# Second MLP stage in tiles of the first stage's pools, and one written order for its engines

## The chip, the cores and the metric

The kernel runs on one core of a Trainium2 chip. The metric is device time in microseconds, the median of several executions; a profile of one further execution shows where its time goes. Engine names are those of the profile: PE is TensorE (matmuls), PEld its weight loads, DVE is VectorE, ACT is ScalarE, POOL is GpSimd, and SP is SyncE, which issues most transfers.

## The reference

One layer of an encoder with 1024 tokens of width 1024: a normalised input projection, a state-space branch and a neighbourhood attention branch side by side, an output projection with residual, and then the MLP, the only part that the change touches:

```
x = x + jnp.concatenate([y_ssm, y_na.astype(y_ssm.dtype)], axis=-1) @ w_out
h = rmsnorm(x, norm_mlp_w)
return x + jnp.square(jax.nn.relu(h @ w_mlp_in)) @ w_mlp_out     # 1024 -> 4096 -> 1024
```

All of it is float32.

## The kernel before, in words

**Split numbers.** Every matmul operand is split into a high half (ACT copies it to the matmul's rounded type) and a low half (value minus high half, by DVE or POOL; `split_to`, L368 to L370). `chain` (L1218 to L1221) then makes three matmuls of one: high by high, high by low, low by high.

**Seven products.** Both MLP multiplications use a scheme of seven products of half-size blocks instead of eight, in the order `ORD = (1, 2, 6, 5, 7, 3, 4)`. Sums of inputs are made ahead of a product, sums of results behind it. In PSUM, products 1, 6, 7 and 4 add up in the tiles X (`px`), products 2 in Y (`py`), 5 and 3 in a second Y (`pz`).

**First stage** (h @ W1, squared ReLU). Eight blocks `fb` of 512 features (class `Block`). A block loads four weight quarters, and per product: `split` makes the sums of weights (L1583 to L1587) and splits them (ACT high, POOL low); `product` issues 24 matmuls; `sums` copies the PSUM tiles into `cq` (ACT, L1628) or adds them there (DVE, L1633), applies relu and square (ACT, L1638 and L1639, L1630), makes the sums of activations that the second stage needs (DVE, L1646 to L1654) and stores seven forms of the activations to DRAM (`act_dr`; from SP, for the last block from POOL). The transposed input `hc` lives in the pools `hA` and `b0`, the blocks' results in four buffers of `hq`.

**Second stage** (times W2, plus residual). Four parts `fb` of 1024 features. A part loads eight weight quarters into `wraw`, and per product: two loads of activations `ar` from `act_dr`; splits of them into `ahl` (ACT high, DVE low, `a_split`); sums of weights (DVE: L1915 and L1916 for products 6 and 5, L1918 for 7, L1920 for 4); splits of two weights (ACT high, POOL low, L370); 48 matmuls in four groups t of 12; and four adds of a PSUM tile to the accumulators `acc` (DVE, L1945). `acc` is loaded with the residual from `x2_dr`. In the last part finished tiles are stored to the output.

**Pools.** Before, the first stage's pools are closed (`b0s.close()`), and the second stage opens ten pools of its own in their memory. Weight splits go round seven pairs, activation splits round six, activation loads round four tiles.

**Order of work.** The stages before the MLP are emitted by planners that set an order, kept by `in_order` (L1188): each instruction gets a dependency, without a semaphore, on the one emitted before it on the same engine. Blocks 0 to 7 of the first stage and the whole second stage are outside `in_order`: there a scheduler of the language, which works with estimated times, chooses the order of each engine's instructions.

Of the kernel before, what the change touches and what calls it, by code (L numbers as in the profile page):

```python
# [19 lines left out]
P = 128  # L20
T = 1024
D = 1024
# [208 lines left out]
def hymba_block(  # L231
# [136 lines left out]
    def split_to(hl, src, eng):  # L368
        nc.scalar.activation(hl[0], src, AF.Copy)  # L369
        eng.tensor_tensor(hl[1], src, hl[0].bitcast(F32), op=sub)  # L370
# [150 lines left out]
    with ExitStack() as ph:  # L521
# [663 lines left out]
        behind = {}  # L1185

        @contextmanager
        def in_order():  # L1188
            traced = nc.cur_bb.bb.instructions
            mark = traced[-1]  # L1190
            yield
            start = next(i for i in reversed(range(len(traced))) if traced[i] is mark) + 1
            for ins in traced[start:]:
                if ins.engine in behind:
                    tc.add_manual_dep(
                        ins,
                        behind[ins.engine].name,
                        mybir.DependencyInfo(
                            mybir.DependencyClass.NoSync, mybir.DependencyReason.DATA
                        ),  # L1200
                        reason="issue_after",
                    )
                behind[ins.engine] = ins
# [342 lines left out]
    with ExitStack() as ph:  # L1546
# [280 lines left out]
        x2s.close()  # L1827
        arp = arps.enter_context(tc.tile_pool(name="arp", bufs=1, reuse_waits="tile"))
        hq = ph.enter_context(tc.tile_pool(name="hq", bufs=1, reuse_waits="tile"))
        for fb in range(8):  # L1830
            kb = (k0, k1)[fb] if fb < 2 else Block(fb)
            kb.load("12", "21", "22")
            kb.tiles()
            for i in ORD:
                if i not in kb.w:
                    kb.split(i)
                if not (i == 1 and fb < 2 or i == 2 and fb == 0):
                    kb.product(i)
                elif i == 1:
                    kb.to = kb.X  # L1840
                else:
                    kb.to = kb.Y
                kb.sums(i)
    b0s.close()

    with ExitStack() as ph:
        phase["ps"] = ph.enter_context(
            tc.tile_pool(name="ps4", bufs=1, space=PSUM, reuse_waits="tile")
        )
        ra, wa_, rb, x0, wb_, a2, a1, arb = (  # L1850
            ph.enter_context(tc.tile_pool(name=n, bufs=1, side="right", reuse_waits="tile"))
            for n in ("ra", "wa", "rb", "x0", "wb", "a2", "a1", "arb")
        )
        x1, a3 = (
            ph.enter_context(tc.tile_pool(name=n, bufs=1, reuse_waits="tile")) for n in ("x1", "a3")
        )
        acc = [p.tile([P, NT // 2, D], F32, name="acc") for p in (x0, x1)]
        hls[:] = [wa_] * 2 + [wb_] * 2 + [wp] * 3
        raw_a = [arp] * 2 + [ra] * 4
        raw_b = [rb] * 6 + [wp] * 2  # L1860
        raw_x = [arp] * 2 + [arb] * 2
        ahl = [a1] * 2 + [a2] * 2 + [a3] * 2
        for n in ("hl", "raw", "rb", "ar", "ahl"):
            ring[n] = 0

        def raw_of(n):
            if n in ("11", "21"):
                return ring_tile("raw", raw_a, ("wraw",), (F32,))[0]
            return ring_tile("rb", raw_b, ("wraw",), (F32,))[0]

        def a_load(fb, i, u):
            ar = ring_tile("ar", raw_x, ("ar",), (F32,))[0]
            nc.sync.dma_start(
                ar.rearrange("p (a t) -> p a t", a=2), act_dr[fb][i - 1, :, 2 * u : 2 * u + 2, :]
            )
            return ar

        def a_split(ar):
            pool = ahl[ring["ahl"] % 6]
            ring["ahl"] += 1  # L1880
            t = pool.tile([P, 2, 1024], F32R, tag="ahl", name="ahl", bufs=2)
            split_to((t[:, 0], t[:, 1]), ar, nc.vector)
            return t[:, 0], t[:, 1]

        for fb in range(4):
            bq = [{}, {}]
            for n in ("11", "21", "12", "22"):
                for q in bq:
                    q[n] = raw_of(n)
            first = {}  # L1890
            with ExitStack() as order:
                if fb == 1:
                    order.enter_context(tc.issue_after(begun.ins))
                for n in ("11", "21", "12", "22"):
                    for u in range(2):
                        r0 = (2 * fb + u) * 512 + (int(n[0]) - 1) * 256
                        d0 = (int(n[1]) - 1) * 512
                        nc.sync.dma_start(
                            bq[u][n].rearrange("p (a d) -> p a d", a=2),
                            w_mlp_out[0][r0 : r0 + 256, d0 : d0 + 512].rearrange(  # L1900
                                "(a p) d -> p a d", p=P
                            ),
                        )
                    if n in ("11", "21"):
                        i = 1 if n == "11" else 2
                        first[i] = [a_load(fb, i, u) for u in range(2)]
            X = [ps_mm("px2") for _ in range(4)]
            Y = [ps_tp("py2"), ps_tp("py2"), ps_s("py2"), ps_s("py2")]
            for i in ORD:
                wa = []  # L1910
                for u in range(2):
                    q = bq[u]
                    if i == 6:
                        q["t1"], q["t2"] = raw_of("t1"), raw_of("t2")
                        nc.vector.tensor_tensor(q["t1"], q["12"], q["11"], op=sub)  # L1915
                        nc.vector.tensor_tensor(q["t2"], q["22"], q["t1"], op=sub)  # L1916
                    elif i == 7:
                        nc.vector.tensor_tensor(q["12"], q["22"], q["12"], op=sub)  # L1918
                    elif i == 4:
                        nc.vector.tensor_tensor(q["21"], q["21"], q["t2"], op=sub)  # L1920
                    src = q[{1: "11", 2: "21", 3: "22", 4: "21", 5: "t1", 6: "t2", 7: "12"}[i]]
                    ar = first[i][u] if i in first else a_load(fb, i, u)
                    wa.append((a_split(ar), w_split(src, nc.gpsimd)))
                if fb == 0 and i in (1, 6):
                    h = i == 6
                    for t in range(4):
                        begun = nc.sync.dma_start(acc[h][:, t, :], x2_dr[4 * h + t])
                if i == 5:
                    Y = [ps_tp("pz2"), ps_tp("pz2"), ps_s("pz2"), ps_s("pz2")]
                for t in range(4):  # L1930
                    pt = (X if i in (1, 6, 7, 4) else Y)[t]
                    ts = slice(t * P, t * P + P)
                    for u in range(2):
                        (ah, al), (wh, wl) = wa[u]
# [7 lines left out]
                    th, dh = {1: (0, 0), 2: (0, 0), 6: (0, 1), 3: (0, 1), 5: (1, 1), 7: (1, 1), 4: (1, 0)}[i]  # L1942
                    tt = 4 * th + t
                    d = acc[th][:, t, dh * 512 : (dh + 1) * 512]
                    nc.vector.tensor_tensor(d, d, pt, op=add)  # L1945
                    if fb == 3 and i in (2, 7, 3, 4):
                        nc.sync.dma_start(
                            out[0, tt * P : (tt + 1) * P, dh * 512 : (dh + 1) * 512], d
                        )
    arps.close()  # L1950


# [42 lines left out]
```

## Time and profile before

| | |
|---|---|
| time, median of 3 runs | 1585.77 us (1585.5 to 1588.29) |
| profiled execution: its time, its span | 1589.21 us, 1587.4 us |
| mean granted TensorE clock | 0.992 |
| busy: PE, DVE, ACT, POOL | 1548.1, 1013.5, 720.9, 730.3 us |
| HBM read, written | 191.51 MB, 89.18 MB |
| first stage's last block, second stage | from about 1226 us and from 1272.55 us of the span |

The span goes from the first to the last instruction of the profiled execution; its time holds 1.8 us more. A row of a timeline gives start, duration, engine, line, operation, output<-inputs, and in brackets how long the engine was idle before and whose instruction ended that. A row of waits gives the total, the number and the longest.

### The profile page before, as it was taken

The numbers are of one execution on the slowest core, as the hardware profiler recorded it, in microseconds if no ns is written. First come the engines' busy times: TensorE is split into PE (matmuls) and PEld (weight loads), VectorE is DVE, ScalarE is ACT, GpSimd is POOL, SyncE is SP. The second block draws the span as 40 slices with busy tenths as digits, with TensorE's granted clock in tenths as the row PEclk, the third lists the DMA queues.
The fourth block names the chain that finished last, engine by engine and source line by source line (L and its number), as shares of the span: only waits on it lengthen the run. The fifth ranks groups of instructions, "written<-read, shape, count | busy, mean of one in ns | idle before, by whom it ended". The sixth has DMA issues, their size and how long they took to land. (4 is left out here: it accounts for less than half of the span.)

```text
span 1587.4 us, 20805 instructions
## 1 busy us (share of the span) xinstructions
PE 1548.1 (98%) x7462; PEld 1291.3 (81%) x7462; DVE 1013.5 (64%) x1414; ACT 720.9 (45%) x1187; POOL 730.3 (46%) x530
## 2 busy tenths in 40 slices
PE   7999999999999999999999998999999999999999
PEld 5788878888878888788888886888888778888887
DVE  3776444687688854567776475444444579787863
ACT  5444323444345435567686244554454444333330
POOL 2000066774779832233364353444444555555450
PEclk9999999999999999999999999999999989999999
DMA  8212398777777795978792422444443486443332
GB/s 225 54 40 70 89 311 262 231 238 248 230 209 214 225 278 172 257 208 227 193 238 94 159 94 93 174 158 146 151 155 120 159 306 251 159 161 131 107 106 80
DMA packets 184226, 278.73 MB, mean 176 GB/s; under 512 B 14819, under 2 KB 106043, under 8 KB 184123
## 3 DMA queue, kind: packets, MB, share of 16 engines
q1 hardware_dynamic: 133323, 233.88, 48.2%
q10 hardware_dynamic: 49792, 39.85, 7.6%
q0 software_dynamic: 1008, 3.67, 0.6%
q8 instruction: 59, 0.97, 0.3%
q14 instruction: 44, 0.36, 0.1%
HBM read 191.51 MB, written 89.18 MB: 177 GB/s over the span
## 5 line engine op out<-in xcount | busy, mean ns | idle before, releaser
L370 POOL TENSOR_TENSOR wl<-wraw,wh 128x1024 fp32r<-128x1024 f32 x113 | 308.7, 2743 | 305.5 <-ACT wh L369 305.5
L364 PE MATMUL pq<-wh,hTh 128*128 128x512 f32 x512 | 204.9, 400 | 2.3 <-DVE qn L931 1.7
L366 PE MATMUL pq<-wh,hTl 128*128 128x512 f32 x512 | 199.9, 390 | 0.0
L365 PE MATMUL pq<-wl,hTh 128*128 128x512 f32 x512 | 199.7, 390 | 0.1
L369 ACT ACTIVATE wh<-wraw 128x1024 fp32r<-128x1024 f32 x125 | 131.4, 1055 | 143.5 <-PE px L1221 40.1
L1221 PE MATMUL px<-wh,ahl 128*128 128x512 f32 x512 | 163.1, 395 | 4.6 <-ACT ahl L369 3.1
L1221 PE MATMUL px<-h,wh 128*128 128x512 f32 x512 | 160.1, 394 | 2.7 <-DVE cq L1633 2.7
L370 DVE TENSOR_TENSOR ahl<-ar,ahl 128x1024 fp32r<-128x1024 f32 x56 | 117.0, 2094 | 22.4 <-ACT ahl L369 21.5
L369 ACT ACTIVATE ahl<-ar 128x1024 fp32r<-128x1024 f32 x56 | 58.5, 1052 | 160.3 <-PE px L1221 80.6
L1221 PEld LDWEIGHTS px<-wh,ahl 128*128 128x128 f32 x512 | 97.6, 191 | 26.7 <-ACT ahl L369 3.6
L1221 PEld LDWEIGHTS px<-h,wh 128*128 128x128 f32 x512 | 96.6, 190 | 22.9 <-DVE cq L1633 3.1
L364 PEld LDWEIGHTS pq<-wh,hTh 128*128 128x128 f32 x512 | 96.2, 188 | 21.8 <-DVE qn L931 2.1
L366 PEld LDWEIGHTS pq<-wh,hTl 128*128 128x128 f32 x512 | 96.1, 188 | 20.8
L365 PEld LDWEIGHTS pq<-wl,hTh 128*128 128x128 f32 x512 | 96.3, 188 | 18.9 <-DVE wl L884 0.5
L1221 PE MATMUL px<-wl,ahl 128*128 128x512 f32 x256 | 101.3, 396 | 0.0
L1221 PE MATMUL px<-h,wl 128*128 128x512 f32 x256 | 100.4, 392 | 0.0
L1439 DVE TENSOR_TENSOR ptl<-ptp,pth 128x384 fp32r<-128x384 f32 (+1 forms) x128 | 65.4, 520 | 37.5 <-ACT pth L1441 36.5
L1405 DVE CUSTOM_DVE_ANT_0 pr<-psc,mb 128x384 f32<-128x384 f32 (+1 forms) x128 | 65.7, 520 | 26.6 <-PE psc L1402 23.5
L1417 ACT ACTIVATE pr<-pr,nmx 128x384 f32<-128x384 f32 (+1 forms) x128 | 74.6, 584 | 17.3 <-DVE nmx L1405 16.8
L1221 PE MATMUL pz<-h,wh 128*128 128x512 f32 x256 | 80.3, 395 | 0.8 <-DVE h L1763 0.8
L364 PE MATMUL po<-wh,yh 128*128 128x512 f32 x192 | 80.1, 417 | 0.2 <-DVE x L1327 0.2
L1221 PE MATMUL pz<-wh,ahl 128*128 128x512 f32 x256 | 80.1, 389 | 0.0
(332 smaller groups left out, 3743.4 us busy)
## 6 DMA issues: line engine op xcount, KB each, us to landing
ar<-act_dr SPq DMA_DIRECT2D x56, 512.0 KB, 4.4
act_dr<-cq SPq DMA_DIRECT2D x49, 512.0 KB, 3.0
wraw<-in_w_in_dram SPq DMA_DIRECT2D x44, 512.0 KB, 6.3
rb<-cum_dr SPq DMA_DIRECT2D x32, 512.0 KB, 6.1
wraw<-in_w_mlp_in_dram SPq DMA_DIRECT2D x32, 512.0 KB, 5.2
wraw<-in_w_mlp_out_dram SPq DMA_DIRECT2D x32, 512.0 KB, 5.6
q_dr<-hl ACTq DMA_DIRECT2D x16, 512.0 KB, 5.6
k_dr<-hl ACTq DMA_DIRECT2D x16, 512.0 KB, 3.6
```

The source lines that it names most:

```text
L364: nc.tensor.matmul(pt, lhsT=ah, rhs=bh, start=first, stop=False)
L365: nc.tensor.matmul(pt, lhsT=ah, rhs=bl, start=False, stop=False)
L366: return nc.tensor.matmul(pt, lhsT=al, rhs=bh, start=False, stop=last)
L369: nc.scalar.activation(hl[0], src, AF.Copy)
L370: eng.tensor_tensor(hl[1], src, hl[0].bitcast(F32), op=sub)
L1221: nc.tensor.matmul(pt, lhsT=a, rhs=b, start=f, stop=l, skip_group_check=True)
L1405: nc.vector.tensor_tensor_reduce(pr.t[:, 0:n], pt.t[:, 0:n], mb.t[:, o : o + n], scale=-1.0, scalar=3.0e38, op0=add, op1=ALU.min, accum_ou ...
L1417: nc.scalar.activation(pr.t[:, 0:n], pr.t[:, 0:n], AF.Exp, bias=nmx.t[:, b : b + 1], scale=-1.0, accum_out=den.t[:, hh, b : b + 1],)
L1439: nc.vector.tensor_tensor(lo[0], pv3, hi.bitcast(F32), op=sub)
```

## The change

The first stage's loop covers blocks 0 to 6. Block 7 and the whole second stage are emitted inside one `in_order(skip=SP)`: PE, DVE, ACT and POOL run the instructions exactly as written, SP's are still ordered by the scheduler. Steps of the second stage's first products are written between those of block 7, and later each product is written with the steps of the product two further on between its four groups (`ready`, a generator).

The second stage opens no pools. It takes tiles by tag from pools that are still open: activation splits from `hA` (tags h1, h2, h3), weight splits from `b0` (k, v, kl) and `wp`, weight sums from `hA` (h7), accumulators from `hA` (h4) and `hq`, activation loads from `arp` and `b0` (q), the first weight quarter from `arp` and `hq`. Weight splits now go round six pairs, activation splits round six, activation loads round two double tiles. The matmuls are the same in kind and number.

Cut to its core:

```
-        def in_order():
+        def in_order(skip=()):
...
             for ins in traced[start:]:
+                if ins.engine in skip:
+                    continue
...
-        for fb in range(8):
+        for fb in range(7):
...
+        rings = {
+            "ahl": [over(hA, f"h{i}{n}") for i in (1, 2, 3) for n in range(2)],
+            "hl": [over(b0, t) for t in ("k", "v", "kl")] + [of_wp] * 3,
+            "raw": [over(arp, "wraw", F32), over(hq, "q", F32)],
+            "ar": [over(arp, "ar", F32), over(b0, "q", F32)],
+            "t": [over(hA, f"h7{n}", F32) for n in range(2)],
+        }
...
+            def ready(self, i, change=True):
+                for u in range(2):
+                    if change:
+                        self.change(i, u)
+                    yield
+                self.split_a(i)
+                yield
+                for u in range(2):
+                    self.split_w(i, u)
+                yield
...
+        with in_order(skip=(mybir.EngineType.SP,)):
+            kb.split(1)
+            kb.split(2)
+            kb.split(6)
+            kb.product(1)
+            kb.sums(1)
+            kb.split(5)
+            kb.product(2)
+            kb.sums(2)
+            kb.split(7)
+            kb.product(6)
+            o.split_a(1)
+            kb.sums(6)
+            o.load_a(2)
+            kb.split(3)
+            kb.product(5)
+            o.split_w(1, 0)
+            kb.sums(5)
+            o.load("12")
+            o.load("22")
+            kb.split(4)
+            kb.product(7)
+            o.split_w(1, 1)
+            o.split_w(2, 0)
+            kb.sums(7)
+            kb.product(3)
+            o.split_a(2)
+            o.split_w(2, 1)
+            kb.sums(3)
+            kb.product(4)
+            o.change(6, 0)
+            o.change(6, 1)
+            kb.sums(4)
+            load_acc(0)
+            row = [(o, i) for i in ORD] + [(p, i) for p in map(Part, range(1, 4)) for i in ORD]
+            for n, (o, i) in enumerate(row):
+                ahead = iter(row[n + 2][0].ready(row[n + 2][1], n > 0) if n + 2 < len(row) else ())
+                for _ in o.product(i):
+                    next(ahead, None)
+                if n == 1:
+                    begun = load_acc(1)
+                    tc_after = begun.ins
+                if i == 5 and o.fb < 3:
+                    row[n + 4][0].load_all(tc_after if o.fb == 0 else None)
```

`kb` is block 7, `o` the second stage's part 0; `change` makes the sums of weights, `split_a` and `split_w` the splits of activations and weights. Lines of the first stage move by 2 (the add L1633 is L1635); the second stage's add L1945 is L1963, its weight sums are L1912 to L1917.

What this does to VectorE's row at block 7: `cq` are the block's results, `px_10963` and `px_10964` its two X tiles, `wraw` weights and `wt` sums of them. Before:

```order
L1915 TENSOR_TENSOR wraw<-wraw 128x1024 x2
L1633 TENSOR_TENSOR cq<-cq,px_10963 128x512
L1916 TENSOR_TENSOR wraw<-wraw 128x1024
L1918 TENSOR_TENSOR wraw<-wraw 128x1024
L1916 TENSOR_TENSOR wraw<-wraw 128x1024
L1918 TENSOR_TENSOR wraw<-wraw 128x1024
L1633 TENSOR_TENSOR cq<-cq,px_10964 128x512
L1633 TENSOR_TENSOR cq<-cq,pz_11079 128x512
L1633 TENSOR_TENSOR cq<-cq,pz_11080 128x512
L1646 TENSOR_TENSOR cq<-cq 128x1024
```

And after, on VectorE in the same place:

```order
L370 TENSOR_TENSOR ahl<-ar,ahl 128x1024 x2
L1589 TENSOR_TENSOR wraw<-wraw 128x1024
L1635 TENSOR_TENSOR cq<-cq,px_10963 128x512
L1635 TENSOR_TENSOR cq<-cq,px_10964 128x512
L370 TENSOR_TENSOR ahl<-ar,ahl 128x1024 x2
L1635 TENSOR_TENSOR cq<-cq,pz_11107 128x512
L1635 TENSOR_TENSOR cq<-cq,pz_11108 128x512
L1648 TENSOR_TENSOR cq<-cq 128x1024
L1650 TENSOR_TENSOR cq<-cq 128x1024
L1652 TENSOR_TENSOR cq<-cq 128x1024
L1912 TENSOR_TENSOR wt<-wraw 128x1024
L1913 TENSOR_TENSOR wt<-wraw,wt 128x1024
```

Four sums of weights stood between the two adds of product 7; now they stand behind the sums of product 3, and four activation splits have come forward.

ScalarE's row at the end of block 7, before:

```order
L369 ACTIVATE wh<-wraw 128x1024 x3
L1638 ACTIVATE cq<-cq 128x1024
L369 ACTIVATE wh<-wraw 128x1024
L1639 ACTIVATE cq<-cq 128x1024
L1638 ACTIVATE cq<-cq 128x1024
L1630 ACTIVATE cq<-px_10963 128x512
L1639 ACTIVATE cq<-cq 128x1024
L369 ACTIVATE wh<-wraw 128x1024
L1630 ACTIVATE cq<-px_10964 128x512
L369 ACTIVATE ahl<-ar 128x1024 x2
```

And ScalarE after, from the split of block 7's product 7 on (`whl` are weight splits in tiles of `b0`):

```order
L369 ACTIVATE wh<-wraw 128x1024
L369 ACTIVATE ahl<-ar 128x1024 x2
L1630 COPY cq<-px_10963 128x512
L1630 COPY cq<-px_10964 128x512
L369 ACTIVATE wh<-wraw 128x1024
L369 ACTIVATE whl<-wraw 128x1024
L1630 COPY cq<-pz_11107 128x512
L1630 COPY cq<-pz_11108 128x512
L369 ACTIVATE wh<-wraw 128x1024
L369 ACTIVATE whl<-wraw 128x1024 x2
L1640 ACTIVATE cq<-cq 128x1024
L1641 ACTIVATE cq<-cq 128x1024
```

The first copies of activations stood last in block 7, behind the reads of its last product; now they stand behind product 6.

GpSimd's row from block 7's first store on, before:

```order
L1619 DMA act_dr_5517<-cq 128x1024
L370 TENSOR_TENSOR wl<-wraw,wh 128x1024 x6
L1619 DMA act_dr_5517<-cq 128x1024 x2
L370 TENSOR_TENSOR wl<-wraw,wh 128x1024
L1619 DMA act_dr_5517<-cq 128x1024 x2
L370 TENSOR_TENSOR wl<-wraw,wh 128x1024 x2
L1619 DMA act_dr_5517<-cq 128x1024 x2
```

And GpSimd after:

```order
L1621 DMA act_dr_5517<-cq 128x1024
L370 TENSOR_TENSOR wl<-wraw,wh 128x1024 x2
L370 TENSOR_TENSOR whl<-wraw,whl 128x1024
L370 TENSOR_TENSOR wl<-wraw,wh 128x1024
L370 TENSOR_TENSOR whl<-wraw,whl 128x1024 x2
L1621 DMA act_dr_5517<-cq 128x1024
L370 TENSOR_TENSOR wl<-wraw,wh 128x1024
L1621 DMA act_dr_5517<-cq 128x1024 x5
L370 TENSOR_TENSOR wl<-wt,wh 128x1024 x2
```

The last five stores now stand together, ahead of the splits for the second stage's product 6.

More of the change, by code (lines that the diff above doesn't have):

```diff
@@ L1843, in hymba_block @@
                 kb.sums(i)
[L1844 to L1894, printed above, removed]
-                    for u in range(2):
[L1896 to L1934, printed above, removed]
@@ new lines, in over, with of_wp @@
+        def over(pool, tag, dt=F32R):
+            return lambda name: pool.tile([P, 2, 1024], dt, tag=tag, name=name, bufs=4 if pool is hq else 1)
+        def of_wp(name):
+            return [wp.tile([P, 1024], F32R, tag=t, name=t, bufs=3) for t in ("wh", "wl")]
+        rings = {
[5 more added lines that the diff above has]
+        }
@@ new lines, in hymba_block, with next_of, __init__, load @@
+        used = dict.fromkeys(rings, 0)
+        def next_of(key, name):
+            n = used[key]
+            used[key] += 1
+            t = rings[key][n % len(rings[key])](name)
+            return t if isinstance(t, list) else (t[:, 0], t[:, 1])
+        acc = {}
+        class Part:
+            def __init__(self, fb):
+                self.fb = fb
+                self.q = [{}, {}]
+                self.ar, self.a, self.w = {}, {}, {}
+            def load(self, n):
+                if n == "11":
+                    both = next_of("raw", "wraw")
+                else:
+                    both = [ring_tile("raw", raws, ("wraw",), (F32,))[0] for _ in range(2)]
+                for u in range(2):
+                    self.q[u][n] = both[u]
+                    r0 = (2 * self.fb + u) * 512 + (int(n[0]) - 1) * 256
+                    d0 = (int(n[1]) - 1) * 512
+                    nc.sync.dma_start(
+                        both[u].rearrange("p (a d) -> p a d", a=2),
+                        w_mlp_out[0][r0 : r0 + 256, d0 : d0 + 512].rearrange(
+                            "(a p) d -> p a d", p=P
+                        ),
+                    )
+            def load_a(self, i):
+                self.ar[i] = next_of("ar", "ar")
+                for u, ar in enumerate(self.ar[i]):
+                    nc.sync.dma_start(
+                        ar.rearrange("p (a t) -> p a t", a=2),
+                        act_dr[self.fb][i - 1, :, 2 * u : 2 * u + 2, :],
+                    )
+            def split_a(self, i):
+                if i not in self.ar:
+                    self.load_a(i)
+                for u in range(2):
+                    hl = next_of("ahl", "ahl")
+                    split_to(hl, self.ar[i][u], nc.vector)
+                    self.a[i, u] = hl
+            def change(self, i, u):
+                q = self.q[u]
+                if i == 6:
+                    q["t1"], q["t2"] = next_of("t", "wt")
+                    nc.vector.tensor_tensor(q["t1"], q["12"], q["11"], op=sub)
+                    nc.vector.tensor_tensor(q["t2"], q["22"], q["t1"], op=sub)
+                elif i == 7:
+                    nc.vector.tensor_tensor(q["12"], q["22"], q["12"], op=sub)
+                elif i == 4:
+                    nc.vector.tensor_tensor(q["21"], q["21"], q["t2"], op=sub)
+            def split_w(self, i, u):
+                n = {1: "11", 2: "21", 3: "22", 4: "21", 5: "t1", 6: "t2", 7: "12"}[i]
+                hl = next_of("hl", "whl")
+                split_to(hl, self.q[u][n], nc.gpsimd)
+                self.w[i, u] = hl
+            def load_all(self, after):
+                with ExitStack() as order:
+                    if after:
+                        order.enter_context(tc.issue_after(after))
+                    for n in ("11", "21", "12", "22"):
+                        self.load(n)
+            def ready(self, i, change=True):
+                for u in range(2):
+                    if change:
[3 more added lines that the diff above has]
+                yield
+                for u in range(2):
+                    self.split_w(i, u)
+                yield
+            def product(self, i):
+                if i == 1:
+                    self.X = [ps_mm("px2") for _ in range(4)]
+                elif i in (2, 5):
+                    n = "py2" if i == 2 else "pz2"
+                    self.Y = [ps_tp(n), ps_tp(n), ps_s(n), ps_s(n)]
+                th, dh = {1: (0, 0), 2: (0, 0), 6: (0, 1), 3: (0, 1), 5: (1, 1), 7: (1, 1), 4: (1, 0)}[i]
+                for t in range(4):
+                    pt = (self.X if i in (1, 6, 7, 4) else self.Y)[t]
+                    for u in range(2):
+                        (ah, al), (wh, wl) = self.a[i, u], self.w[i, u]
@@ L1941, in hymba_block @@
                             )
-                    th, dh = {1: (0, 0), 2: (0, 0), 6: (0, 1), 3: (0, 1), 5: (1, 1), 7: (1, 1), 4: (1, 0)}[i]
                     tt = 4 * th + t
-                    d = acc[th][:, t, dh * 512 : (dh + 1) * 512]
+                    d = acc[tt // 2][:, tt % 2, dh * 512 : (dh + 1) * 512]
                     nc.vector.tensor_tensor(d, d, pt, op=add)
-                    if fb == 3 and i in (2, 7, 3, 4):
+                    if self.fb == 3 and i in (2, 7, 3, 4):
                         nc.sync.dma_start(
@@ L1949, in hymba_block, with load_acc @@
                         )
+                    yield
+        def load_acc(h):
+            for n in range(2):
+                acc[2 * h + n] = t = over(*((hA, f"h4{n}"), (hq, "q"))[h], F32)("acc")
+                for m in range(2):
+                    last_ = nc.sync.dma_start(t[:, m], x2_dr[4 * h + 2 * n + m])
+            return last_
+        kb, o = Block(7), Part(0)
+        kb.load("12", "21", "22")
+        kb.tiles()
+        o.load("11")
+        o.load_a(1)
+        o.load("21")
+        with in_order(skip=(mybir.EngineType.SP,)):
[42 more added lines that the diff above has]
+                    row[n + 4][0].load_all(tc_after if o.fb == 0 else None)
+    b0s.close()
     arps.close()
```

## The prediction

> **What bounds the kernel now.** I read the page first, then TensorE's waits, then the timeline of the one place where it waits late in the kernel, then the groups of the last stage. The page says which engine has the time:
>
> ```profile
> PE 1548.1 (98%) x7462; PEld 1291.3 (81%) x7462; DVE 1013.5 (64%) x1414; ACT 720.9 (45%) x1187; POOL 730.3 (46%) x530
> ```
>
> TensorE is busy for 98% of 1587.4 us, so only idle or slow stretches of TensorE can be won, not work on another engine. Its waits from 980 us on, the two MLP stages, are only these:
>
> ```profile
> PE px L1221 <- ACT ahl L369: 3.1, 1, 3.1
> PE px L1221 <- DVE cq L1633: 2.7, 1, 2.7
> PE px L1221 <- DVE ahl L370: 1.5, 2, 0.8
> ```
>
> Four waits, 7.3 us. All lie where the last block of the first stage hands over to the second stage. TensorE's timeline there (start, us, instructions, idle time before in brackets; rows between are left out):
>
> ```profile
> 1261.74 0.39 PE L1221 MATMUL px<-h,wl 128*128 128x512 f32 x1
> 1264.82 1.12 PE L1221 MATMUL px<-h,wh 128*128 128x512 f32 x2 [2.69 <-DVE cq L1633]
> 1265.74 0.63 PE L1221 MATMUL px<-h,wl 128*128 128x512 f32 x1
> 1266.16 1.05 PE L1221 MATMUL px<-h,wh 128*128 128x512 f32 x2
> ...
> 1269.04 0.39 PE L1221 MATMUL px<-h,wl 128*128 128x512 f32 x1
> 1272.55 0.79 PE L1221 MATMUL px<-wh,ahl 128*128 128x512 f32 x1 [3.12 <-ACT ahl L369]
> ...
> 1277.16 1.22 PE L1221 MATMUL px<-wh,ahl 128*128 128x512 f32 x2 [0.83 <-DVE ahl L370]
> ...
> 1325.33 0.73 PE L1221 MATMUL px<-wh,ahl 128*128 128x512 f32 x2 [0.69 <-DVE ahl L370]
> ```
>
> The idle time is half of the loss. After the wait of 2.69 us the starts are 0.43 us apart (1265.74 to 1266.16), and the granted clock of this stretch is the second row here (stretch, its length, busy time and instructions of each engine, PEclk):
>
> ```profile
> 1226.61:1264.69 38.08, 35.52 (x157) 29.10 (x155) 23.25 (x14) 14.79 (x18) 22.91 (x9) 1.00 0.53 193
> 1264.69:1284.35 19.66, 15.58 (x42) 11.49 (x42) 15.43 (x10) 13.38 (x15) 13.83 (x10) 0.65 0.71 268
> 1344.21:1420.37 76.16, 76.16 (x338) 63.09 (x337) 63.25 (x54) 27.35 (x29) 42.76 (x14) 1.00 0.51 167
> ```
>
> Full speed is read in the chain that ended last, once the second stage runs:
>
> ```profile
> 1376.85 10.88 PE px L1221 x48
> ...
> 1572.69 10.89 PE px L1221 x48
> 1583.59 0.02 issue
> 1583.61 0.69 DVE acc L1945
> ```
>
> A product of 48 matmuls takes 10.88 us, 0.2267 us each. So the whole loss can be counted. After the matmul of 1261.74 the next could start at 1261.97. Twelve matmuls of the first stage were left (2.72 us), so the second stage could begin at 1264.69; it began at 1272.55: 7.86 us. Its 28 products need 28 x 10.88 = 304.64 us, and it ran from 1272.55 to 1583.58, 311.03: 6.39 us more. Of the 14.25 us I take off 0.16, by which the last matmul's shown duration (0.39) is longer than its pace. **The prize is 14.1 us**: about 7.6 waiting, 6.5 slow clock.
>
> **What sets these waits.** VectorE, ScalarE and GpSimd ahead of the handover:
>
> ```profile
> 1253.54 2.82 DVE L1916 TENSOR_TENSOR wraw<-wraw 128x1024 f32<-128x1024 f32 x1
> 1256.28 3.42 DVE L1918 TENSOR_TENSOR wraw<-wraw 128x1024 f32<-128x1024 f32 x1
> 1259.62 3.42 DVE L1916 TENSOR_TENSOR wraw<-wraw 128x1024 f32<-128x1024 f32 x1
> 1262.96 1.21 DVE L1918 TENSOR_TENSOR wraw<-wraw 128x1024 f32<-128x1024 f32 x1
> 1264.09 0.67 DVE L1633 TENSOR_TENSOR cq<-cq,px 128x512 f32<-128x512 f32 x1
> ...
> 1249.53 12.42 POOL L370 TENSOR_TENSOR wl<-wraw,wh 128x1024 fp32r<-128x1024 f32 x4 [3.03 <-ACT wh L369]
> ...
> 1264.80 1.06 ACT L1638 ACTIVATE cq<-cq 128x1024 f32<-128x1024 f32 x1 [7.27 <-DVE cq L1633]
> ...
> 1271.45 1.99 ACT L369 ACTIVATE ahl<-ar 128x1024 fp32r<-128x1024 f32 x2
> ```
>
> VectorE does four weight differences of the second stage (L1916, L1918) ahead of the add at 1264.09 that reads px. Product 4 of the last block writes that px, so its second half waits. ScalarE stands 7.27 us behind the same add and then does a backlog before its first copies of activations at 1271.45, for which TensorE waits again at 1272.55. The halves that VectorE makes after those are the third wait. It is one chain, and it begins with VectorE's order.
>
> **The change part by part.** *Last block, order.* Now VectorE does both adds of product 7 right behind the first split of activations, and the weight differences behind the sums of product 3. The second add can run when product 7 is done: the block began 156 matmuls before 1261.97, at 1226.61, and five products of 5.44 us end at 1253.8, the add at 1254.5; product 4 needs it at 1259.25. The first wait goes, with 4.7 us to spare. ScalarE's first copies stand ahead of product 3's split, at about 1242 instead of 1271.45, and the third wait goes with them.
>
> What is late next? I lay out the written order with these durations:
>
> ```profile
> 1237.76 0.69 DVE L1633 TENSOR_TENSOR cq<-cq,py 128x512 f32<-128x512 f32 x1 [2.05 <-PE py L1221]
> 1266.88 2.40 POOL L370 TENSOR_TENSOR wl<-wraw,wh 128x1024 fp32r<-128x1024 f32 x1 [4.93 <-ACT wh L369]
> 1283.66 2.35 DVE L370 TENSOR_TENSOR ahl<-ar,ahl 128x1024 fp32r<-128x1024 f32 x2
> 1288.20 2.47 DVE L1945 TENSOR_TENSOR acc<-acc,px 128x512 f32<-128x512 f32 x4
> ```
>
> So 1.2 us for a VectorE operation of 128x1024 beside an idle GpSimd, 0.67 for an add out of PSUM, 2.4 for a GpSimd subtraction, 1.06 for a ScalarE copy, 0.95 in a run.
>
> First, the weights of product 3, last block. Sum of product 2 done 1238.45; ScalarE: two steps, the split of product 7 and two activation copies, to 1243.4. VectorE: two low halves, the first behind GpSimd's split of product 7 (to 1244.1), and the difference for product 3, to 1247.6. ScalarE's copy to 1248.7, GpSimd's subtraction to 1251.1. Due 1253.8: 2.7 us spare. Product 4's split is third in GpSimd's row then, 1251.1 + 2 x 2.4 = 1255.9, due 1259.25: 3.3 spare.
>
> Second, product 6 of the second stage, due at 1264.69 + 21.76 = 1286.45, its second input half six matmuls later, 1287.8. VectorE's low halves for product 2 stand beside three GpSimd subtractions and end at 1263.1; two adds to 1264.5; ScalarE's relu and square to 1266.6; then three sums, four differences, one sum (8 x 1.2) to 1276.2, with GpSimd idle because its stores wait for those sums in the written order; three adds to 1278.2; two low halves, each behind one GpSimd subtraction (2 x 3.4) to 1285. That is 2.8 us spare, and GpSimd's own two subtractions end earlier. The last block's two accumulators are read by ScalarE right after its square, by 1268.5; the second stage's third tile needs the first of them at 1270.1: 1.6 spare.
>
> So four places have 1.6 to 3.3 us each: the likeliest loss is none. The row of 1325.33 shows that a small miss is cheap: 0.69 of idle time, and two matmuls in 0.73.
>
> *Steady second stage.* No step is added: per part 14 GpSimd and 14 ScalarE weight splits, 14 activation splits, 28 adds, 8 differences as before. The matmuls are the same. Buffers are about as deep: low and high halves for three products before and after, four activation loads under way. A part takes 76.16 us of TensorE at a granted clock of 1.00 with VectorE 63.25 busy (row above). In the written order splits come two products (21.76 us) ahead, and the longest VectorE list, product 1 with four differences, ends about 16 us into these 21.76.
>
> *Queue of loads.* SyncE is exempt from the written order; the loads of weights for the third and fourth part are drawn forward on it. A blocked load holds those behind it; I found none that waits for a step less than 20 us ahead of its own reader.
>
> *End.* The last add and the stores of the output are the same: 1583.61 to 1587.4 stays.
>
> **Sum.** Profiled execution: span 1587.4 - 14.1 = 1573.3, its time 1589.21 - 14.1 = 1575.1. The median, 1585.77, lies 3.4 below that execution. I keep back 0.4 us, half the wait at 1325.33, for a narrow place missed: 1585.77 - 13.7 = **1572.1**.
>
> **Two rules weighed.** The groups of the last stage:
>
> ```profile
> L370 DVE TENSOR_TENSOR ahl<-ar,ahl 128x1024 fp32r<-128x1024 f32 x56 | 117.0, 2094 | 22.4 <-ACT ahl L369 21.5
> L370 POOL TENSOR_TENSOR wl<-wraw,wh 128x1024 fp32r<-128x1024 f32 x52 | 153.1, 2964 | 125.1 <-ACT wh L369 125.0
> ```
>
> A VectorE operation takes 1.2 us alone and 3.42 beside GpSimd (1259.62). This is a rival of its own, A. If the written order puts every one of a part's 14 subtractions in front of a VectorE operation, VectorE needs 28 x 0.68 + 22 x 1.2 + 14 x 2.2 = 76.2 us a part, as much as TensorE's 76.16. It then paces the end of each part, some 0.5 us four times: 1574. Against: VectorE waits for adds while GpSimd works, so they alternate. Chance 0.05. [...]
>
> On the clock: 2.69 us of waiting were followed by twelve matmuls at up to 0.43 us. [...] The measured rows decide: a wait of 2.7 us costs some 1.7 more.
>
> **Rivals.** *B, the handover keeps a wait.* One of the four places is missed by 3 us, for instance because a load lands late on the full queue. Price as at 1264.82: 2.85 + 1.7 = 4.6 us, so 1576.3; two of them, 1581. For it: the stretch from 1264.69 has a DMA share of 0.71. Chance 0.20.
>
> *C, slower: the activation loop.* In the written order VectorE stands still at a split whose load is late, and the adds behind it with it. A buffer pair is now refilled only when both halves are split.
>
> ```profile
> ar<-act_dr SPq DMA_DIRECT2D x54, 512.0 KB, 4.4
> 1309.71 1.06 ACT L369 ACTIVATE ahl<-ar 128x1024 fp32r<-128x1024 f32 x1 [8.87 <-DMA ar<-act_dr]
> ```
>
> One round of the pair: landing of two loads (4.4 and, at the 167 to 268 GB/s of the stretches above, some 2.5 more), two copies 2.0, two low halves up to 6.8: 15.7 us. It may last two products, 21.76. It decides when the pair needs more than 12.9 us instead of 6.9; with 15 us each of the 13 rounds is 2.1 us late, +27, less 14.1: 1599. For it: 1309.71, where ScalarE waited 8.87 us for such a load. Against: TensorE did not wait then, and before had the same four tiles. Chance 0.08.
>
> *D, nothing changes*, because SyncE's order undoes it or the scheduler had no choice: 1585.8. Against: the differences stand behind the adds in the new order. Chance 0.03.
>
> **Chances and range.** The forecast, 1571.4 to 1573, has 0.64, A 0.05, B 0.20, C 0.08, D 0.03. The range goes from 1570.2 (the lowest run shown, 1585.5, less 14.1, and 1.2 for the spread between runs) to 1578.5, which takes in A and most of B and leaves out C, D and the worse B. About 0.2% (3.2 us) is what a measurement of this kernel can tell from no change. Faster by more: the forecast, A, B: 0.89. Within: D, 0.03. Slower: C, 0.08.
>
> **What would show it.** Right: no wait of TensorE over 1 us after 980; granted clock 1.00 from 1226 to the end; the second stage starts at about 1264.7 and ends 304.8 later. Wrong: waits of TensorE on a GpSimd subtraction before products 3 or 4 of the last block, on VectorE's low half before product 6 (B); a wait at each part's product 6 or first product (A); ScalarE waiting for act_dr loads in every product (C).

## The result and the profile after

The changed kernel takes 1571.73 us (median of 4 runs, 1570.84 to 1574.24) against 1585.63 (4 runs, 1583.2 to 1588.29) of the kernel before on the same chip: a ratio of 0.9915, 95% interval 0.9895 to 0.9934. The forecast was 1572.1.

The profiled execution took 1570.84 us, span 1569.0. The busy times on its page:

```profile
PE 1540.5 (98%) x7462; PEld 1286.4 (82%) x7462; DVE 1001.3 (64%) x1414; ACT 723.7 (46%) x1187; POOL 715.3 (46%) x530
```

The number of instructions of every engine is the same; the work is in another order, and partly in other tiles. TensorE's waits from 980 us on, four rows before, are an empty list now. The chain that ended last shows the handover (start, us, matmuls; a piece runs to the end of its last matmul, so the next one starts 0.16 us later than in a timeline):

```profile
1243.39 5.44 PE px L1223 x24
1248.83 5.44 PE pz L1223 x24
1254.27 16.32 PE px L1223 x72
1270.59 10.88 PE py L1223 x48
1281.47 0.45 PE px L1223 x2
1281.92 0.04 issue
1281.96 10.73 PE px L1223 x46
```

The third row holds product 4 of the first stage's last block and product 1 of the second stage, 24 + 48 matmuls in 16.32 us, which is 72 at full pace: the place where 2.69 and 3.12 us of waiting stood. One hitch is left, at 1281.9. The windows say the same (the last block; the second stage's first two products; one later part):

```profile
1221.50:1259.55 38.05, 38.05 (x170) 31.50 (x169) 17.48 (x14) 22.23 (x26) 24.19 (x11) 1.00 0.55 199
1259.55:1281.31 21.76, 21.76 (x98) 18.02 (x97) 20.26 (x12) 11.19 (x13) 12.41 (x10) 1.00 1.02 340
1335.71:1411.87 76.16, 76.16 (x338) 63.08 (x337) 56.57 (x51) 28.15 (x29) 37.47 (x14) 1.00 0.42 138
```

TensorE is busy for the whole of each, at a granted clock of 1.00; before, the stretch behind the last block had 0.65.

**One yardstick for all runs.** Block 7 and the second stage are 1512 matmuls, 63 times 24. At 5.44 us each and with 0.16 for the longer last one they need 342.88 us. What a trace shows from block 7's first matmul to the end of the last one, less 342.88, I call its loss:

| kernel | first matmul of block 7 | last one's end | loss |
|---|---|---|---|
| before | 1226.61 | 1583.57 | 14.08 |
| after | 1221.47 | 1564.69 | 0.34 |

Loss accounts for 13.74 us, and the medians differ by 13.9. The two spans differ by 18.4: block 7 also began 5.14 us earlier, behind stages that the change leaves alone, and 0.5 us more pass between the last matmul and the end. The first MLP matmul begins anywhere from 936.8 to 945.8 us in the eleven profiles of this study, so experiments are compared by loss first and by median second. Each loss is read from one profiled execution; how far it differs between executions of one kernel was not measured. The ratios compare with runs of the kernel before that were made beside the experiments, in three sets with medians of 1583.52, 1585.49 and 1585.38 us; a ratio is not always the quotient of the two medians. One run of the first experiment, 2203.21 us long at a granted clock of 0.656, is left out of its figures.

### The profile page after: what moved, and what is told of

Its sections match the earlier page's. It is cut to its first block, busy times and chain, and to the rows that moved or that the text cites. A ratio compares the mean times of both kernels' runs of the same rounds, so it can differ in the third digit from the quotient of the medians.

```text
span 1569.0 us, 20786 instructions
## 1 busy us (share of the span) xinstructions
PE 1540.5 (98%) x7462; PEld 1286.4 (82%) x7462; DVE 1001.3 (64%) x1414; ACT 723.7 (46%) x1187; POOL 715.3 (46%) x530
## 4 chain that ended last, share of the span: by engine, by line
PE 87%; DMA 4%; DVE 3%; issue 2%; POOL 2%; ACT 1%; SPq 0%; ACTq 0%; POOLq 0%; DVEq 0%
PE px L1223 22%; PE pz L1223 11%; PE pq L364 6%; PE pq L365 6%; PE pq L366 6%; PE py L1223 5%; PE po L365 3%; PE po L364 3%; PE po L366 3%; PE px L364 3%; PE px L365 3%; PE px L366 3%; PE pv L1371 2%; PE ptp L1431 2%; PE pd L1128 2%
## 5 line engine op out<-in xcount | busy, mean ns | idle before, releaser
L370 POOL TENSOR_TENSOR wl<-wraw,wh 128x1024 fp32r<-128x1024 f32 x76 | 192.9, 2541 | 205.5 <-ACT wh L369 205.3
L369 ACT ACTIVATE wh<-wraw 128x1024 fp32r<-128x1024 f32 x88 | 92.6, 1059 | 142.1 <-PE px L1223 29.1
L370 DVE TENSOR_TENSOR ahl<-ar,ahl 128x1024 fp32r<-128x1024 f32 x56 | 108.6, 1978 | 7.3 <-ACT ahl L369 7.3
L1223 PE MATMUL px<-whl,ahl 128*128 128x512 f32 x408 | 96.5, 389 | 0.0
L1223 PEld LDWEIGHTS px<-whl,ahl 128*128 128x128 f32 x408 | 76.6, 188 | 15.9
L370 POOL TENSOR_TENSOR whl<-wraw,whl 128x1024 fp32r<-128x1024 f32 x21 | 57.8, 2762 | 63.2 <-ACT whl L369 62.9
L1223 PE MATMUL px<-wh,ahl 128*128 128x512 f32 x240 | 77.9, 390 | 0.0
```

What stands on the lines that cost most here:

```text
L1223: nc.tensor.matmul(pt, lhsT=a, rhs=b, start=f, stop=l, skip_group_check=True)
```

## The experiments

**Each half of the new order, undone.** In the changed kernel VectorE's four weight sums go back ahead of the adds of product 7:

```
             kb.product(7)
             o.split_w(1, 1)
             o.split_w(2, 0)
+            o.change(6, 0)
+            o.change(6, 1)
             kb.sums(7)
...
             kb.product(4)
-            o.change(6, 0)
-            o.change(6, 1)
```

> After, with the four sums of weights for product 6 written ahead of the adds of product 7, as VectorE had them before. Theory: product 4 of block 7 waits for the first of these adds. The last weight quarter was issued at 1250.78 in the trace of after and lands some 5.6 us later, so the last sum ends at 1257.6 or later and the first add at 1258.3, where product 4 is due at 1254.1: a wait of about 4 us and 1.7 to 2.5 of slow clock, 1577 to 1579. Rival (the pools make the gain, order is nothing): within 0.2% of after, 1569 to 1575.

Measured: 1579.62 us (1576.95 to 1580.93), ratio to the kernel before 0.9962 (0.9943 to 0.9982), loss 8.69. That is just above the theory's range, since the wait is 6.16 us and not about 4. VectorE there, then TensorE:

```profile
1249.77 2.94 DVE L1912 TENSOR_TENSOR wt<-wraw 128x1024 f32<-128x1024 f32 x1 [6.49 <-PE px L1223]
1252.74 3.30 DVE L1913 TENSOR_TENSOR wt<-wraw,wt 128x1024 f32<-128x1024 f32 x1
1255.97 3.36 DVE L1912 TENSOR_TENSOR wt<-wraw 128x1024 f32<-128x1024 f32 x1
1259.36 1.23 DVE L1913 TENSOR_TENSOR wt<-wraw,wt 128x1024 f32<-128x1024 f32 x1
1260.50 1.28 DVE L1635 TENSOR_TENSOR cq<-cq,px 128x512 f32<-128x512 f32 x2
```

```profile
1261.33 1.19 PE L1223 MATMUL px<-h,wh 128*128 128x512 f32 x2 [6.16 <-DVE cq L1635]
```

Three of the sums take about 3 us beside GpSimd, and the first add of product 7, for which product 4 waits, ends at about 1261.1 (the last row holds both). This is the first wait of before, longer since here both adds stand behind the sums; before, one stood ahead of them. Nothing else waits up to the end.

The other half: the first splits of activations go back behind the last block.

```
             kb.product(6)
-            o.split_a(1)
             kb.sums(6)
...
             kb.sums(4)
+            o.split_a(1)
             load_acc(0)
```

> After, with the split of the first activations (two ScalarE copies, two VectorE low halves) written behind all of block 7. Theory: the copies end at about 1265, the low halves at 1271.7 behind VectorE's sums; in the written order TensorE's third matmul of the second stage needs a low half and is due at 1260.0, so it waits 11 to 12 us in two pieces, with 2 to 3 us of slow clock: 1584 to 1588, no better than before. Rival (pools): within 0.2% of after.

Measured: 1583.14 us (1579.72 to 1590.85), ratio 0.9988 (0.9968 to 1.0008), loss 11.57. The two waits make 8.9 us, less than the 11 to 12 of the theory. TensorE, then ScalarE and VectorE:

```profile
1271.46 0.74 PE L1223 MATMUL px<-whl,ahl 128*128 128x512 f32 x2 [2.72 <-ACT ahl L369]
1278.33 6.04 PE L1223 MATMUL px<-whl,ahl 128*128 128x512 f32 x16 [6.13 <-DVE ahl L370]
```

```profile
1270.37 1.99 ACT L369 ACTIVATE ahl<-ar 128x1024 fp32r<-128x1024 f32 x2
...
1277.06 2.35 DVE L370 TENSOR_TENSOR ahl<-ar,ahl 128x1024 fp32r<-128x1024 f32 x2
```

Most of the gain is gone, though the add of product 7 is in time. The copies stand behind ScalarE's reads of the last product, and the low halves, 6.7 us later, behind VectorE's four weight sums. So the second and third wait come back with the early splits alone taken away; they do not need the first.

**Half of the new order, put into the kernel before.** The four sums are held there behind product 7's adds; all else is left to the scheduler.

```
+                        self.added = nc.vector.tensor_tensor(c, c, pt, op=add)
+                        if i == 7:
+                            self.last7 = self.added
...
+                    held = ExitStack()
+                    if fb == 0 and i in (6, 7):
+                        held.enter_context(tc.issue_after(kb.last7.ins))
...
+                    held.close()
```

> Before, pools and scheduler as they were, with one thing added: VectorE's sums of weights for the second stage's products 6 and 7 of part 0 are held behind the adds of product 7 of block 7. Theory: the wait of 2.7 us and its slow clock are gone (4.6 us); ScalarE is no longer behind that add, but its first copies still stand behind the reads of block 7's last product, and VectorE's low halves behind the sums, so 4 to 9 us of the 14 stay: 1576 to 1581. Rival (pools): the same as before within 0.2%.

A miss: 1585.62 us (1577.31 to 1589.9), ratio 0.9992 (0.997 to 1.0014), loss 12.93. VectorE and ScalarE:

```profile
1260.27 3.08 DVE L1921 TENSOR_TENSOR wraw<-wraw 128x1024 f32<-128x1024 f32 x1
1263.28 1.21 DVE L1923 TENSOR_TENSOR wraw<-wraw 128x1024 f32<-128x1024 f32 x1
1264.41 0.68 DVE L1633 TENSOR_TENSOR cq<-cq,pz 128x512 f32<-128x512 f32 x1
...
1265.12 1.06 ACT L1640 ACTIVATE cq<-cq 128x1024 f32<-128x1024 f32 x1
...
1268.59 1.99 ACT L369 ACTIVATE ahl<-ar 128x1024 fp32r<-128x1024 f32 x2
```

```profile
1269.69 0.80 PE L1221 MATMUL px<-wh,ahl 128*128 128x512 f32 x1 [6.24 <-ACT ahl L369]
```

The first wait is gone. But the sums now stand among product 3's adds (1264.41), ScalarE's relu waits for those, and its first copies begin 43.4 us behind block 7's start, against 44.8 before. TensorE comes earlier to the second wait and stands there 6.24 us instead of 3.12. That could be my choice of place, so the sums were held behind product 3's adds as well (`if i == 3`).

> The kernel before, with VectorE's sums of weights for the second stage's products 6 and 7 held until the add of product 3 (the last add of the last block), where the earlier try held them only until product 7's add and left product 3's adds among the sums. Theory 1, the loss at the handover is one chain that begins with VectorE's order: no wait on an add (cq), product 3's adds end by about 1260, ScalarE stands at its relu and square by 1261 and the loss of the MLP's second half falls from 14.2 us to under 6; 1575 to 1578. Theory 2, ScalarE's place for the first copies of activations is a cause of its own (they stand behind the two reads of the last product, which cannot end before about 1262): the first wait goes, a wait of 2 to 4 us of TensorE on ahl stays at the first matmul of the second stage, with some 2 us of slow clock and the small waits behind it: a loss of 7 to 10 us, 1578 to 1582.

Measured: 1584.92 us (1579.03 to 1589.92), ratio 0.9999 (0.9984 to 1.0013), loss 13.87. Both theories miss; the second was right that a wait on the copies stays, neither foresaw the larger one behind it. TensorE, then VectorE:

```profile
1262.74 0.50 PE L1221 MATMUL px<-wh,ahl 128*128 128x512 f32 x1 [1.63 <-ACT ahl L369]
1274.34 1.22 PE L1221 MATMUL px<-wh,ahl 128*128 128x512 f32 x2 [9.49 <-DVE ahl L370]
```

```profile
1256.31 2.35 DVE L1920 TENSOR_TENSOR wraw<-wraw 128x1024 f32<-128x1024 f32 x2
...
1261.99 3.42 DVE L1921 TENSOR_TENSOR wraw<-wraw 128x1024 f32<-128x1024 f32 x1
1265.34 3.37 DVE L1923 TENSOR_TENSOR wraw<-wraw 128x1024 f32<-128x1024 f32 x1
1268.63 3.38 DVE L1650 TENSOR_TENSOR cq<-cq 128x1024 f32<-128x1024 f32 x1
1271.93 1.21 DVE L1652 TENSOR_TENSOR cq<-cq 128x1024 f32<-128x1024 f32 x1
1273.07 1.21 DVE L370 TENSOR_TENSOR ahl<-ar,ahl 128x1024 fp32r<-128x1024 f32 x1
```

Now every add is in time and ScalarE has copied by 1263.6, but VectorE does nine sums (six of weights, three of activations) from 1256.31 on, three of them at 3.4 us, before the first low half. The wait has moved a second time, each time to the next step that product 1 of the second stage needs: add, copy, low half. Moving the sums back gains nothing while the splits stay last.

**Where the written order is needed.** The changed kernel, its tiles and its sequence, but no written order at all:

```
-        with in_order(skip=(mybir.EngineType.SP,)):
+        with nullcontext():
```

> Pools and sequence of emission as after, but the scheduler again chooses each engine's order from block 7 on. In its order the two adds of product 7 have one sum of weights between them (not four), and ScalarE's first copies of activations still stand early. Theory (the place of these steps decides, not the strictness of the order): no wait of TensorE over 1.5 us at the handover, 1571 to 1576. Rival (the fixed order itself is what pays): the waits of before return, 1580 to 1586.

Measured: 1577.6 us (1575.09 to 1581.28), ratio 0.9964 (0.9944 to 0.9983), loss 7.39: between the two expectations. Block 7 loses nothing, as the theory had it; the largest waits lie inside the second stage:

```profile
1332.63 11.12 PE L1223 MATMUL px<-whl,ahl 128*128 128x512 f32 x48 [1.75 <-DVE acc L1963]
1345.71 1.63 PE L1223 MATMUL px<-whl,ahl 128*128 128x512 f32 x6 [1.96 <-DVE acc L1963]
```

TensorE waits for a px tile that VectorE's add has not yet given back. So by the losses about half of the gain comes with tiles that are open early and the sequence of emission, which were not tried apart, and half with the written order. Which half of that order? Here only block 7 is written, and the second stage is the scheduler's (the lines from `row =` on moved out of the `with`):

> The changed kernel with the written order kept for the last block of the first stage alone; the second stage is emitted in the same sequence from the same tiles, but the scheduler chooses its order. Theory 1, the written order is needed at the handover alone: no wait over 0.5 us, 1571 to 1573. Theory 2, the scheduler's own order costs inside the second stage, as in the run with no written order at all, where 6.9 us were lost, all of them after 1268: waits of TensorE on VectorE's adds to the accumulators between 1290 and 1355, 4 to 7 us in all, 1576 to 1579.

Measured: 1573.17 us (1571.67 to 1576.86), ratio 0.9934 (0.9911 to 0.9957), loss 0.93. The first theory holds, but for one wait of a little more than 0.5 us:

```profile
1286.77 0.50 PE L1223 MATMUL px<-wl,ahl 128*128 128x512 f32 x1 [0.64 <-POOL wl L370]
```

By this loss, written order in block 7 is enough; the medians cannot tell this kernel from the changed one. The waits at 1332 and 1345 of the run before do not appear, though the second stage was left to the scheduler in both. The traces show where the two part. VectorE in the run without a written order:

```profile
1283.65 10.89 DVE L370 TENSOR_TENSOR ahl<-ar,ahl 128x1024 fp32r<-128x1024 f32 x1
...
1309.94 1.23 DVE L1912 TENSOR_TENSOR wt<-wraw 128x1024 f32<-128x1024 f32 x1 [5.49 <-DMA wraw<-in_w_mlp_out_dram]
```

There a low half took 10.89 us, as long as four GpSimd subtractions of 2.4 us and its own 1.2 (an estimate of what held it). The next low half came behind it, and a load of activations that waited for that one was issued at 1296.29; behind it on SyncE, from 1298.08, followed the second part's weights from their second quarter on, which are issued from 1282.15 here. VectorE waited 5.49 us for one of them, and its sums and adds were late from there to the two waits. That the one low half began this is read from the trace and was not tested.

**What the look-ahead is worth.** In the changed kernel the steps of the next product, not of the one after it, are written between a product's groups:

```
-                ahead = iter(row[n + 2][0].ready(row[n + 2][1], n > 0) if n + 2 < len(row) else ())
+                ahead = iter(row[n + 1][0].ready(row[n + 1][1], n > 1) if 0 < n < len(row) - 1 else ())
```

> After, with the steps of the next product instead of the next but one among a product's groups. Theory: plain products still arrive in time (low halves end 10.0 and 11.1 us after the product before begins, due 11.3 and 12.7), products 7 and 4 are some 0.7 us late, product 6 with its four sums 3 to 5 us and the clock with it, in three parts: 1585 to 1600. Rival (one product of look-ahead is enough): within 0.2% of after. Rival (the loop of activation loads paces): a wait at every product, over 1610.

Measured: 1608.31 us (one run), loss 30.87; more than the theory expected. Its waits:

```profile
PE px L1223 <- DVE ahl L370: 10.1, 14, 1.4
PE px L1223 <- POOL wl L370: 5.4, 7, 0.8
PE px L1223 <- POOL whl L370: 3.3, 4, 0.8
```

25 waits, none over 1.4 us, spread over all four parts. Product 6 loses 3.6 to 6.2 us with its slow clock, about as reckoned; the theory was wrong on products 7 and 4, which lose 2.0 us, and not 0.7, nearly every time. Within the written order, the second product of look-ahead alone holds more than the whole handover.

And the kernel before with its second stage's own sequence as the written order (`in_order(skip=SP)` around the four parts), in which a product's splits stand directly ahead of it:

> Before, with its second stage in a written order, that of its own source: the steps of a product directly ahead of its matmuls, nothing of the next product among them. Pools as before. Theory (the look-ahead in the sequence pays, an order without it costs): VectorE begins the next product's low halves behind the last add, 1.4 us late for products 1, 2, 5 and 3, about 6 for 7 and 4 (sum, copy, subtraction in a row), about 9 for 6: 27 us a part, with slow clock 32, so 1690 to 1730. Rival (a fixed order pays by itself): 1572 to 1580.

Measured, as expected: 1724.47 us (one run), loss 155.12. The two largest groups of its waits:

```profile
PE px L1223 <- ACT wh L369: 44.4, 13, 4.3
PE px L1223 <- POOL wl L370: 43.7, 26, 2.8
```

They lie as reckoned: 4.3, 2.5 and 1.6 us in a row at product 6, some 6 us at products 7 and 4, 1.5 at the others. A fixed order is no gain by itself: the same tool costs 139 us where the sequence has no look-ahead.

**The hitch at 1281.9.** In the changed kernel the activations of product 6 are split before the four weight sums instead of behind them:

```
-                self.split_a(i)
+                if change:
+                    self.split_a(i)
...
             kb.product(4)
+            o.split_a(6)
             o.change(6, 0)
```

The first change keeps `ready` from splitting product 6 of part 0 a second time.

> After, with the activation split of the second stage's product 6 written ahead of the four sums of weights instead of behind the first three accumulator adds. In the trace of after one low half took 9.7 us there, while GpSimd ran four subtractions back to back, and TensorE waited 0.2 us for it. Theory (a VectorE operation can stand behind a whole run of GpSimd subtractions): with GpSimd idle the two low halves take 1.2 us each, TensorE's wait of 0.2 us is gone and the time is the same as after within 0.2%. Rival (the 9.7 us are the load or the copy being late): the low halves are still late and the wait stays or grows.

Measured: 1570.15 us (1568.02 to 1573.66), ratio to the kernel before 0.9904 (0.9866 to 0.9942), loss 0.00. The low halves of product 6 on VectorE:

```profile
1268.14 2.35 DVE L370 TENSOR_TENSOR ahl<-ar,ahl 128x1024 fp32r<-128x1024 f32 x2
```

With GpSimd idle the two take 2.35 us together, as the theory had it. The hitch is gone from the trace, and block 7 and the second stage run at full pace from end to end. The medians of this kernel and the changed one cannot be told apart by these runs.

## Why the prediction was right

**The prize.** Forecast 14.1 us, 0.4 kept back; the loss went from 14.08 to 0.34. Both were read from the pace of TensorE, which is why the total fits although steps below were wrong. The signs named for a right forecast came: no wait in the list, granted clock 1.00; the second stage began at 1259.55, which is 38.08 behind block 7's start as forecast, and ended 305.1 later (304.8 expected). That the median came within 0.4 us of the forecast is in part luck: the interval of the ratio alone reaches from 1569.0 to 1575.2 us. The forecast's split of the prize, 7.6 waiting and 6.5 slow clock, is a little off its own rows, whose four waits add up to 7.3.

**The layout by hand.** Block 7 begins 5.14 us earlier in this trace than in the one that the forecast was laid out on. These are rows of VectorE (two), ScalarE and GpSimd after. With 5.14 added, the second puts product 3's weight sum at an end of 1247.5, where the forecast had 1247.6:

```profile
1248.93 0.69 DVE L1635 TENSOR_TENSOR cq<-cq,px 128x512 f32<-128x512 f32 x1 [2.04 <-PE px L1223]
...
1241.16 1.21 DVE L1589 TENSOR_TENSOR wraw<-wraw 128x1024 f32<-128x1024 f32 x1
...
1236.34 1.99 ACT L369 ACTIVATE ahl<-ar 128x1024 fp32r<-128x1024 f32 x2
...
1248.35 2.41 POOL L370 TENSOR_TENSOR wl<-wraw,wh 128x1024 fp32r<-128x1024 f32 x1
```

Product 4's weights on GpSimd end at 1250.76 + 5.14 = 1255.9, as forecast to the tenth. The last add of product 7 ends at 1249.6 and product 4 begins at 1254.1: 4.5 spare, forecast 4.7. This place had even more: the last add belongs to the second of the two X tiles, and in before twelve matmuls of product 4 ran ahead of the wait for it. The first copies begin at 1236.34 + 5.14 = 1241.5, forecast about 1242.

**The mis-sized step: "two low halves, each behind one GpSimd subtraction (2 x 3.4)".** There was no spare at product 6; it came some 0.2 us late. VectorE and GpSimd there:

```profile
1272.21 10.83 DVE L370 TENSOR_TENSOR ahl<-ar,ahl 128x1024 fp32r<-128x1024 f32 x2
...
1271.35 4.78 POOL L370 TENSOR_TENSOR wl<-wt,wh 128x1024 fp32r<-128x1024 f32 x2
1276.08 4.73 POOL L370 TENSOR_TENSOR whl<-wt,whl 128x1024 fp32r<-128x1024 f32 x2
```

Four GpSimd subtractions ran back to back, 2.4 us each, to 1280.8, and the first low half, begun at 1272.21, ended only behind the fourth: 9.70 us for it, 1.21 for the second. The third matmul of product 6 reads this first low half and was due at 1281.76; the half ended at 1281.91. With 3.4 us for it the forecast had it 5.3 us early, and its 2.8 us of spare looked at the second half alone. It cost 0.3 us, which the 0.4 kept back for a narrow place covered. At 2.4 us each, two more subtractions in the run would have made it some 5 us late, an estimate: rival B.

**"It is one chain, and it begins with VectorE's order" failed.** The forecast did not need it for its sum, but it was the explanation given. With VectorE's order mended alone (in the kernel before, two ways) the loss stays at 12.93 and 13.87; with it right and only the first splits late, it is 11.57. There are two causes, each enough for more than half of the loss: VectorE's sums ahead of the adds (8.69 alone, there ahead of both adds), and the place of the second stage's first splits behind the last block (11.57 alone). They overlap, since TensorE waits once for whichever ends last: holding back the sums alone takes 1.2 us at most off the loss of 14.08, and early splits alone, in the tiles and the order of the changed kernel, 5.4. Whether the early splits would do in the tiles of before was not tried: by the source they use pools there that are opened only behind the last block.

**Steady second stage, and the rivals.** No wait after 1282, as forecast. VectorE is busy 56.57 us of a part's 76.16, so it paces nothing (A). The low halves take less time on average than before (1978 ns over all 56, against 2094); in the second stage:

```profile
L370 DVE TENSOR_TENSOR ahl<-ar,ahl 128x1024 fp32r<-128x1024 f32 x52 | 100.0, 1963 | 0.0
L369 ACT ACTIVATE ahl<-ar 128x1024 fp32r<-128x1024 f32 x52 | 53.9, 1055 | 96.0 <-PE pz L1223 33.4 <-DMA ar<-act_dr 33.1 <-PE px L1223 19.4
```

ScalarE does wait for loads of activations, 33.1 us over the stage, as rival C had it, but VectorE is never idle ahead of a low half (the 0.0 of the first row), so it does not stand still at a split as C needs. The run with one product ahead lost 30.5 us more, about C's size, but not by its mechanism: ScalarE waited 75.2 us for loads there, VectorE still 0.0 ahead of a low half, and TensorE waited for low halves and weight splits that stood behind adds and sums. D is out.

## What to carry to other kernels

When a handover shows several waits in a row, list for each the step that would be late next if it were gone: here add, copy and low half were all late together, and mending the first of them left the time as it was. Tiles that can be taken before the earlier stage has ended, with a sequence that puts the next stage's first steps inside the last block, brought about half of the gain without any fixed order; a fixed order holds such a sequence in place, and it holds a bad one as firmly. And read a loss from the pace of the bound engine, which gives the total even while its cause is misread.

## What the runs showed of the hardware

**VectorE can be kept out by a whole run of subtractions.** In before and after most low halves beside GpSimd took 3.4 us at most, about one subtraction of 2.4 and their own 1.2. Of 148 VectorE operations of 128x1024 behind 980 us, none in before and one in the changed kernel took longer than 3.7 us: the 9.70 above, beside four subtractions. In the run without a written order one such operation took 10.89, at 1283.65; with product 6 split early two low halves took 5.97 together, at 1283.03, beside two subtractions (1281.99, 4.78 us). So VectorE can stand behind more than one GpSimd instruction; what decides it, the runs do not show. Adds with one input from PSUM were not held up: the 158 of them behind 980 us took 0.67 to 0.69 us each, in before and in the changed kernel. So did one beside two subtractions in the run with product 6 split early, VectorE, then GpSimd:

```profile
1279.71 0.69 DVE L1964 TENSOR_TENSOR acc<-acc,py 128x512 f32<-128x512 f32 x1 [0.30 <-PE py L1223]
...
1277.27 4.80 POOL L370 TENSOR_TENSOR wl<-wt,wh 128x1024 fp32r<-128x1024 f32 x2
```

**The clock's price hardly grows with the wait.** Matmuls at 0.43 us instead of 0.2267 followed waits of 2.69 (before), 6.16 (sums first), 6.13 (splits last) and 9.49 us (sums behind product 3). Slow matmuls cost 2.2 to 2.4 us behind each of the last three, and 1.7 behind the first, up to the next wait. A single wait of 1.83 us also cost 1.7. It was in the kernel before with its sums behind product 7, TensorE and the windows of the wait and of what followed:

```profile
1320.24 0.73 PE L1221 MATMUL px<-wh,ahl 128*128 128x512 f32 x2 [1.83 <-DVE ahl L370]
```

```profile
1318.00:1320.20 2.20, 0.41 (x2) 0.00 (x0) 2.20 (x2) 0.93 (x1) 2.20 (x2) 1.00 0.86 333
1320.20:1324.50 4.30, 4.26 (x13) 3.37 (x14) 4.30 (x3) 0.00 (x0) 2.23 (x1) 0.66 0.71 227
```

The clock is still 1.00 in the wait and falls behind it, to 0.66. A wait of 1.96 us in the run without a written order (1345.71) had no such sequel. So below 2 us it can go either way. In the clock records of before and of the changed kernel the slow stretches behind 900 us, but for the one at the very end of each, last 3.4 us, and one of before, at 1271.8, 10.2 us.
